# Up stage of a transformer block: the first weights in other places, the second feature-row set's first unit second, the second norm's subtractions on VectorE

## The chip, the cores and the metric

The kernel runs on one core of one Trainium2 chip. The metric is the device time in microseconds (us) of one execution. The engines are called as in the profile: PE is TensorE (matmuls), PEld its weight loads, DVE is VectorE, ACT is ScalarE, POOL is GpSimd, SP is SyncE, which here issues DMAs. Each engine works through its own instructions in order; between engines there are semaphores.

## The reference

One block with 2048 tokens of width 1024: a first norm and a mixer (two kinds of linear recurrences, in both directions), then a second norm and a feed-forward net whose gate half runs through a convolution of width 3 along the tokens. Everything is in float32. What matters here is the second half:

```
x = x + g1 * (mix_x @ w_out)
hx2 = rmsnorm(x, norm2_g) * (1.0 + sc2) + sh2
gate, up = split(hx2 @ w_up, 2)                 # 2 x 2816 columns
gate = sum(shift(gate, j) * conv_w[j]) + conv_b
x = x + g2 * ((silu(gate) * up) @ w_down)
out = rmsnorm(x, final_g)
```

## The kernel before

Products are made in float16 pairs: a float32 block is split into a high and a low half, and each product of two blocks is three matmuls (function `mm3`, lines 101 to 103). On top of that, the products of 2 x 2 blocks go by a Strassen-Winograd scheme with seven products instead of eight. So each set of features (of 1024 tokens) and each set of weights is held as seven blocks, numbered 0 to 6, each a pair.

The stages in order: `setup` and `heads` (the mixer), `out_proj`, `ffn_up`, `ffn_down`. The change touches the second and the third.

`out_proj` makes the second product and the second norm. Its four `out_product` calls each make 512 tokens of x, scale the rows by their root mean square (L1408, with the factor from a chain of small steps on GpSimd) and leave them in SBUF. Two of them make one feature-row set: `second_norm_a` takes the first 512 tokens of a set, `second_norm_b` the second 512. Both transpose on TensorE (L411), modulate on ScalarE (`modulated`, L1414), make block differences on VectorE (L1441) and split into a pair (`feat_pair`: the high half on ScalarE, L1417; the low half by a subtraction on the engine that is handed in, L1418). `second_norm_a` makes blocks 0 and 1 and keeps what the other blocks need; `second_norm_b` makes blocks 2 to 6. For the second set (t = 1) its two temporary rows lie in the four places with the tag q, and the rows it transposes lie in the places Q0, Q1, FG and KTt.

`ffn_up` runs over 11 pairs of column blocks (j). Each pair has two halves, ty = 0 (gate) and ty = 1 (up), and each half meets two feature-row sets t. One such meeting, (j, ty, t), is a unit (`ffn_unit`): seven products of 12 matmuls of 512 columns, in the order 0, 1, 5, 6, 4, 3, 2, with steps of the scheme's sums between them (ScalarE copies, L592; VectorE sums, L626). A gate unit's four results go through `gate_evac`: ScalarE's scale and bias (L1607), VectorE's two convolution steps (L1612, L1613) and the edges between the 512-token pieces (L1618, L1619). An up unit's go through `up_evac` (one VectorE step, L1632). `act_pairs` then splits the result into seven blocks and stores them in DRAM (L1642 to L1644).

The weights of a half are made by `up_weights(j, ty)`, a generator: load two raw blocks (L1521, two places with the tag wr); square them on ScalarE into the places of the last two blocks (L1528); sum the squares over rows on TensorE (L1533) and derive a power-of-two scale on VectorE; then seven steps, each with ScalarE's cast (L691) and VectorE's remainder (L692), with block differences on GpSimd (L536 to L545) between them. The seven blocks lie in places with the tag z, of which there are 14. The out projection's weights lie in 12 of these 14 until its last product is done. The tag vg (the mixer's value weights had it) has 7 places; later they hold parts of `down_blocks` and the outgoing pieces of `act_pairs`.

`ffn_unit` holds its sums in one buffer for t = 0 (tag ou0, a single place) and in two q places for t = 1. The results `act` of (j, t) lie in three pairs of places, taken in turn by 2j + t: K0 and K1, Q0 and Q1, FG and KTt.

The order is written by hand: while a unit's steps are traced, `work(n)` takes n steps from a list of background generators, `bg`. `ahead(u)` runs only the first step of a generator, its loads. The order in which the code is traced is a priority, not the order of execution: a scheduler with a simulated clock then puts each engine's instructions in a row, taking the first that it holds ready. Before, the units go (0,0,0), (0,0,1), (0,1,0), (0,1,1), (1,0,0), ..., and the list at the start of the up stage is second_norm_b of the second set, the loads of weights (0,1), and then weights (0,1) themselves.

Of the kernel before, what the change touches and what calls it, by code (L numbers as in the profile page):

```python
# [9 lines left out]
F32 = mybir.dt.float32  # L10
F16 = mybir.dt.float16
# [7 lines left out]
P = 128  # L19
# [3 lines left out]
G = 512  # L23
# [5 lines left out]
NJ = NF // 2  # L29
# [9 lines left out]
KEPT = ("K0", "K1", "Q0", "Q1", "FG", "KTt", "ou0")  # L39
# [11 lines left out]
def view(t, off, dims):  # L51
    return bass.AP(t.tensor, t.offset + off, [t.ap[0]] + dims)


class Kern:
# [286 lines left out]
    def modulation(self, cpool, pool, gain, sc, sh, dqcol, room=1.0):  # L342
# [5 lines left out]
        B = cpool.tile(shp, F32, name=f"B{dqcol}")  # L348
        U = pool.tile(shp, F32, tag="ra", bufs=4, name="modu")
        nc.vector.tensor_scalar(U, sc, 1.0, None, ALU.add)  # L350
        nc.vector.tensor_tensor(U, U, gain, ALU.mult)
        j = pool.tile(shp, F32, tag="ra", bufs=4, name="modj")
# [291 lines left out]

    def fm(self, W, X, n):

        def mm(ps, m, start, stop=True, w=None):
            w = W[m if w is None else w]
            for k in range(4):
                self.mm3(ps, lambda q: w[:, q, k], lambda q: X[m][:, k, q], start and k == 0, stop and k == 3)  # L650
        return mm, [P, n]

    def tm(self, W, X, n):

        def mm(ps, m, start, stop=True, w=None):
            w = W[m if w is None else w]
            for i in range(n // P):
# [26 lines left out]

    def pair_blocks(self, raws, W, s, neg, eng):

        nc = self.nc

        def emit(m, v):
            sc = neg if m == 3 else s  # L690
            nc.scalar.activation(W[m][:, 0], v, AF.Copy, scale=sc)  # L691
            nc.vector.scalar_tensor_tensor(W[m][:, 1], v, sc, W[m][:, 0], ALU.mult, ALU.subtract)  # L692
# [727 lines left out]
    def second_norm_a(self, t, xa):  # L1420

        place = (2, 4, 0, 3, 1, 5, 6) if t == 0 else (11, 12, 9, 8, 10, 7, 13)
        X = self.feats[t] = [None] * 7
        for m in (5, 3, 0, 1):
            X[m] = self.slot_tile([P, 4, 2, G], F16, f"y{place[m]}", "feat")
        self.held = [X[m].rearrange("p k a t -> p k (a t)").bitcast(F32) for m in (5, 3)]
        for k in range(4):
            for r in range(2):
                f = self.held[r][:, k]
                self.modulated(f, k + 4 * r, xa)  # L1430
                self.feat_pair(X[r][:, k], f, self.nc.gpsimd)
        self.rest = place

    def second_norm_b(self, t, xb):

        nc = self.nc
        X = self.feats[t]
        for m in (2, 4, 6):
            X[m] = self.slot_tile([P, 4, 2, G], F16, f"y{self.rest[m]}", "feat")
        pair = self.feat_pair  # L1440
        sub = lambda o, x, y: nc.vector.tensor_tensor(o, x, y, ALU.subtract)  # L1441
        for k in range(4):
            if t == 0:
                f = self.slot_tile([P, 2, G], F32, ("ou0", "FG", "KTt")[k % 3], "ftmp")
                b12, b22 = f[:, 0], f[:, 1]
            else:
                b12, b22 = (self.slot_tile([P, G], F32, "q", "ftmp") for _ in range(2))
            b11, b21 = (h[:, k] for h in self.held)
            self.modulated(b12, k, xb)
            self.modulated(b22, k + 4, xb)  # L1450
            yield
            sub(b11, b12, b11)
            pair(X[2][:, k], b22, nc.gpsimd)
            pair(X[4][:, k], b11, nc.vector)
            sub(b12, b22, b12)
            pair(X[6][:, k], b12, nc.gpsimd)
            sub(b22, b22, b11)
            sub(b12, b22, b21)
            pair(X[5][:, k], b22, nc.vector)
            pair(X[3][:, k], b12, nc.vector)  # L1460
            yield

    def out_proj(self):
        self.mod2 = self.modulation(self.cp, self.kp, self.sv[:, V_N2:V_N2 + 8], self.modT[:, 0, 32:40],
                                    self.modT[:, 0, 24:32], 1, 4.0)
        self.feats = [None, None]
        x0 = self.out_product(0)
        self.mixed_pairs(1)
        self.mixed_pairs(2)
        self.second_norm_a(0, x0)  # L1470
        x1 = self.out_product(1)
        self.mixed_pairs(3)
        for _ in self.second_norm_b(0, x1):
            pass
        x2 = self.out_product(2)
        self.ffn_setup()
        self.bg = [self.up_weights(0, 0)]
        self.work(99)
        self.second_norm_a(1, x2)
        x3 = self.out_product(3)  # L1480
        self.bg = [self.second_norm_b(1, x3)]


    def work(self, n):
# [29 lines left out]
    def up_weights(self, j, ty):  # L1514

        nc, kp = self.nc, self.kp
        wup = self.I["w_up"][0].rearrange("(k p) n -> p k n", p=P)
        raw = []
        for f in (j, j + NJ):
            r = self.slot_tile([P, KT, P], F32, "wr", "wur")  # L1520
            nc.sync.dma_start(r, wup[:, :, ty * FF + f * P:ty * FF + (f + 1) * P])  # L1521
            raw.append(r)
        yield
        W = [self.slot_tile([P, 2, 4, P], F16, "z", "w7") for _ in range(7)]
        ssq = kp.tile([P, 2], F32, tag="ssqw2", bufs=2, name="ssqw")
        sqs = [W[5 + i].rearrange("p a k n -> p (a k n)").bitcast(BF16) for i in range(2)]
        for i in range(2):
            nc.scalar.activation(sqs[i], raw[i].rearrange("p k n -> p (k n)"), AF.Square, scale=4.0, accum_out=ssq[:, i:i + 1])  # L1528
        yield
        col = self.ps("sc", [P, 2], "col")  # L1530
        for i in range(2):
            for k in range(KT):
                nc.tensor.matmul(col[:, i:i + 1], sqs[i][:, k * P:(k + 1) * P], self.onesb, start=k == 0 and i == 0,  # L1533
                                 stop=k == KT - 1 and i == 1, skip_group_check=True)
        s, neg, dq = self.scales(self.allsum16(ssq, "sc"), self.dqx[:, 1:2], ("dqz", "dqvg")[ty])

        if ty == 0:
            tap = kp.tile([P, 2, 3], F32, tag="taps", bufs=2, name="taps")
            nc.vector.tensor_scalar(tap, view(self.cw, j, [[NJ, 2], [NF, 3]]), dq, None, ALU.mult)
            row = kp.tile([P, 2], F32, tag="row", bufs=2, name="row")  # L1540
            nc.vector.scalar_tensor_tensor(row, col, 1.0 / 16, view(self.a2, j, [[NJ, 2]]), ALU.mult, ALU.mult)
            nc.vector.tensor_tensor(row, row, view(self.c2, j, [[NJ, 2]]), ALU.add)
            self.rows[j] = row
            self.W[j, 0] = W, tap
        else:
            row = self.rows.pop(j)
            q = kp.tile([P, 2], F32, tag="wdq", bufs=4, name="q")
            nc.vector.tensor_scalar(q, col, self.xx, 1.0, ALU.mult, ALU.mult)
            nc.vector.tensor_tensor(q, q, row, ALU.mult)
            nc.vector.tensor_tensor(q[:, 0:1], q[:, 0:1], q[:, 1:2], ALU.max)  # L1550
            sa, ia = self.pow2(kp, q[:, 0:1], 1, "a")
            nc.vector.tensor_copy(self.sas[:, j:j + 1], sa)
            nc.vector.tensor_copy(self.ias[:, j:j + 1], ia)
            self.W[j, 1] = W, dq
        yield

        yield from self.pair_blocks(raw, W, s, neg, nc.gpsimd)
# [90 lines left out]
    def ahead(self, steps):  # L1648

        next(steps)  # L1650
        yield

    def ffn_up(self):
        U = self.up_weights(0, 1)
        self.bg.append(self.ahead(U))
        for j in range(NJ):

            self.bg.append(U)
            act = [[self.slot_tile([P, 2 * G], F32, KEPT[2 * ((2 * j + t) % 3) + f], "act") for f in range(2)] for t in range(2)]
            ends = [{}, {}]  # L1660
            U = self.up_weights(j + 1, 0)
            for ty in range(2):
                if j + 1 < NJ and ty:
                    self.bg.append(U)
                    U = self.up_weights(j + 1, 1)
                    self.bg.append(self.ahead(U))
                for t in range(2):
                    evac = self.gate_evac(j, t, act, ends) if ty == 0 else self.up_evac(j, t, act)
                    for _ in self.ffn_unit(self.W[j, ty][0], self.feats[t], evac, t):
                        self.work(2)  # L1670
                    if ty == 0 and t == 0:
                        self.bg += [self.ahead(U)] * (j + 1 < NJ) + [self.down_blocks(j)]
                    if ty == 1:
                        self.bg.append(self.act_pairs(j, t, act[t]))
                if ty == 0:
                    self.work(99)
        self.work(99)

    def down_weights(self, m, n):
# [212 lines left out]
```

## Time and profile before

| | |
|---|---|
| time, median of 3 runs | 2640.04 us (2639.76 to 2642.20) |
| span of the profiled execution | 2636.4 us |
| mean granted TensorE clock | 0.981 |
| TensorE busy | 2515.8 us, 95% of the span |
| VectorE busy | 1887.8 us, 72% |
| ScalarE busy | 1349.2 us, 51% |
| GpSimd busy | 425.2 us, 16% |

The span goes from the first to the last instruction of one execution; no other time is listed for that execution. It is 3.6 us under the median. The matmuls overlap each other, so a share of busy time near 100% means that TensorE never waits, not that it could do nothing faster. The granted clock is a share of full speed: at 0.5 each matmul takes twice as long. In the profile the up stage's matmuls are those with feat and w as inputs, from 1391 us on, and those of the down stage are called pd, from 2226 us on.

### The profile page before, as it was taken

Reading aid. Unit: us, or ns where it says so; the run is one execution under the profiler, and the core shown is the slowest. Engines: PE = TensorE matmul, PEld = TensorE weight load, DVE = VectorE, ACT = ScalarE, POOL = GpSimd, SP = SyncE. Lnnn points to the kernel's source line nnn. Section 1 sums busy time; section 2 is a strip of 40 time slices with the busy share of each in tenths; the row PEclk is TensorE's granted clock in tenths of the full one; section 3 lists DMA queues with packets and bytes.
Section 4 is the critical chain, followed back from the end, with each engine's and each line's share of the span. In section 5 each row is a group of like instructions: output and inputs, shape, how many; then the busy total and the mean of one; then the engine's idle time right before and its main releaser. Section 6 shows DMA issues by size and latency. Waiting matters only on the chain. (4 is left out here: it accounts for less than half of the span.)

```text
span 2636.4 us, 56190 instructions
## 1 busy us (share of the span) xinstructions
PE 2515.8 (95%) x22763; PEld 1656.9 (63%) x22763; DVE 1887.8 (72%) x4275; ACT 1349.2 (51%) x2877; POOL 425.2 (16%) x409
## 2 busy tenths in 40 slices
PE   6799998999999999988998999999999999999998
PEld 3678887889899999984454444444444444444443
DVE  4888686786878778675558778888888887323656
ACT  5886466564654454453556556565555555211220
POOL 1100000000000000000354334343434433000000
PEclk7999999999999999998999999999999999999999
DMA  8324342441548567555421332333233236544552
GB/s 295 121 95 162 124 142 85 135 152 67 177 161 291 210 210 255 189 198 192 143 81 41 116 106 99 112 107 110 101 116 120 96 113 225 206 165 159 210 206 87
DMA packets 213621, 393.97 MB, mean 149 GB/s; under 512 B 15600, under 2 KB 97748, under 8 KB 208753
## 3 DMA queue, kind: packets, MB, share of 16 engines
q1 hardware_dynamic: 203808, 373.42, 40.8%
q10 hardware_dynamic: 9248, 16.79, 1.9%
q8 instruction: 178, 2.92, 0.5%
q14 instruction: 83, 0.67, 0.1%
q0 software_dynamic: 304, 0.17, 0.0%
HBM read 298.57 MB, written 91.75 MB: 148 GB/s over the span
## 5 line engine op out<-in xcount | busy, mean ns | idle before, releaser
L101 PE MATMUL pa<-feat,w 128*128 128x512 f16 x704 | 265.0, 381 | 7.6 <-ACT ta L592 5.6
L102 PE MATMUL pa<-feat,w 128*128 128x512 f16 x704 | 267.9, 381 | 0.0
L103 PE MATMUL pa<-feat,w 128*128 128x512 f16 x704 | 267.3, 380 | 0.0
L102 PE MATMUL pd<-wd,actl 128*128 128x512 f16 x616 | 233.3, 379 | 0.0
L103 PE MATMUL pd<-wd,actl 128*128 128x512 f16 x616 | 233.3, 379 | 0.0
L101 PE MATMUL pd<-wd,actl 128*128 128x512 f16 x616 | 232.6, 379 | 0.0
L102 PEld LDWEIGHTS <-w 128*128 128x128 f16 x1232 | 120.9, 98 | 150.9 <-issue 13.0
L103 PEld LDWEIGHTS <-w 128*128 128x128 f16 x1232 | 121.0, 98 | 147.0 <-issue 3.2
L101 PEld LDWEIGHTS <-w 128*128 128x128 f16 x1232 | 120.9, 98 | 141.9 <-issue 3.1
L102 PEld LDWEIGHTS <-hx 128*128 128x128 f16 x1824 | 179.4, 98 | 7.7 <-issue 5.9
L1407 POOL TENSOR_TENSOR ssq<-ssq 128x1 f32<-128x1 f32 x16 | 4.7, 292 | 1102.8 <-ACT junk L1405 1102.8
L101 PEld LDWEIGHTS <-hx 128*128 128x128 f16 x1824 | 179.9, 99 | 2.2
L103 PEld LDWEIGHTS <-hx 128*128 128x128 f16 x1824 | 179.6, 99 | 0.9
L1642 ACT ACTIVATE st<-act,modT 128x512 f16<-128x512 f32 x154 | 107.4, 717 | 109.6 <-DVE act L1632 64.1
L1643 DVE SCALAR_TENSOR_TENSOR st<-act,modT,st 128x512 f16<-128x512 f32 x154 | 140.3, 946 | 29.7 <-ACT st L1642 28.8
L101 PE MATMUL pa<-w_vg,hx 128*128 128x128 f16 x800 | 141.8, 219 | 1.1 <-ACT ct L592 0.7
L102 PE MATMUL pa<-w_vg,hx 128*128 128x128 f16 x800 | 141.7, 219 | 0.0
L103 PE MATMUL pa<-w_vg,hx 128*128 128x128 f16 x800 | 141.7, 219 | 0.0
L101 PE MATMUL pc<-feat,w 128*128 128x512 f16 x352 | 134.8, 383 | 2.2 <-ACT feat L1417 1.3
L103 PE MATMUL pc<-feat,w 128*128 128x512 f16 x352 | 135.2, 384 | 0.0
L102 PE MATMUL pc<-feat,w 128*128 128x512 f16 x352 | 135.0, 383 | 0.1
L101 PE MATMUL pa<-hx,w_z 128*128 128x256 f16 x464 | 127.0, 274 | 1.6 <-DVE K L634 1.3
(552 smaller groups left out, 7357.3 us busy)
## 6 DMA issues: line engine op xcount, KB each, us to landing
hx<-hxd SPq DMA_DIRECT2D x212, 512.0 KB, 4.7
actd<-st SPq DMA_DIRECT2D x154, 256.0 KB, 2.0
actl<-actd SPq DMA_DIRECT2D x28, 1024.0 KB, 5.0
wur<-in_w_up_dram SPq DMA_DIRECT2D x44, 512.0 KB, 3.8
raw<-in_w_in_dram SPq DMA_DIRECT2D x36, 512.0 KB, 4.7
wm<-in_w_mod_dram SPq DMA_DIRECT2D x64, 256.0 KB, 3.7
hxd<-hx SPq DMA_DIRECT2D x28, 512.0 KB, 3.9
wdb<-in_w_down_dram SPq DMA_DIRECT2D x44, 256.0 KB, 3.8
```

The lines of the kernel that those rows point to most:

```text
L101: mm(ps, lhs(0), rhs(0), start=start, stop=False, skip_group_check=True)
L102: mm(ps, lhs(0), rhs(1), start=False, stop=False, skip_group_check=True)
L103: mm(ps, lhs(1), rhs(0), start=False, stop=stop, skip_group_check=True)
L1407: nc.gpsimd.tensor_tensor(ssq[:, 0:1], ssq[:, 0:1], ssq[:, 1:2], ALU.add)
L1642: nc.scalar.activation(p[:, 0], v, AF.Copy, scale=s)
L1643: nc.vector.scalar_tensor_tensor(p[:, 1], v, s, p[:, 0], ALU.mult, ALU.subtract)
```

## The change

The first weights, (0, 0), lie in the vg places instead of z; all others stay in z. The loads of weights (1, 0) are traced before second_norm_a of the second set. In the up stage the units of the first two pairs go (0,0,0), (1,0,0), (0,0,1), (0,1,0), (0,1,1), (1,0,1), (1,1,0), (1,1,1); from the third pair on they go as before. The background list starts with weights (1, 0), then the loads of weights (0, 1), then second_norm_b; weights (0, 1) follow from the second unit on, the down blocks of pair 0 after the third unit, those of pair 1 after the sixth. All 32 low-half subtractions of the second norm that were GpSimd's are VectorE's: 16 in second_norm_a and 16 in second_norm_b.

```diff
@@ second_norm_a
-                self.feat_pair(X[r][:, k], f, self.nc.gpsimd)
+                self.feat_pair(X[r][:, k], f, self.nc.vector)
@@ second_norm_b
-            pair(X[2][:, k], b22, nc.gpsimd)
+            pair(X[2][:, k], b22, nc.vector)
             pair(X[4][:, k], b11, nc.vector)
             sub(b12, b22, b12)
-            pair(X[6][:, k], b12, nc.gpsimd)
+            pair(X[6][:, k], b12, nc.vector)
@@ out_proj
         self.bg = [self.up_weights(0, 0)]
         self.work(99)
+        self.u10 = self.up_weights(1, 0)
+        next(self.u10)
         self.second_norm_a(1, x2)
         x3 = self.out_product(3)
-        self.bg = [self.second_norm_b(1, x3)]
+        self.norm_b = self.second_norm_b(1, x3)
@@ up_weights
-        W = [self.slot_tile([P, 2, 4, P], F16, "z", "w7") for _ in range(7)]
+        W = [self.slot_tile([P, 2, 4, P], F16, "z" if j or ty else "vg", "w7") for _ in range(7)]
@@ ffn_up
-        U = self.up_weights(0, 1)
-        self.bg.append(self.ahead(U))
-        for j in range(NJ):
...
+        u10, u01 = self.u10, U(0, 1)
+        self.bg = [u10, ahead(u01), self.norm_b]
+        unit(0, 0, 0)
+        self.bg.append(u01)
+        unit(1, 0, 0)
+        u11 = U(1, 1)
+        self.bg.append(ahead(u11))
+        unit(0, 0, 1)
+        self.work(99)
+        self.bg.append(self.down_blocks(0))
+        unit(0, 1, 0)
+        unit(0, 1, 1)
+        self.work(99)
+        u20, u = U(2, 0), U(2, 1)
+        self.bg += [u11, ahead(u20)]
+        unit(1, 0, 1)
+        self.work(99)
+        self.bg += [u20, ahead(u), self.down_blocks(1)]
+        unit(1, 1, 0)
+        unit(1, 1, 1)
+        for j in range(2, NJ):
...
```

In the new code `unit(j, ty, t)` does what the inner loop's body did before: it takes the act places, runs `ffn_unit` with `work(2)` after each step, and puts act_pairs on the list after an up unit. The loop from j = 2 keeps the order of before.

More of the change, by code (lines that the diff above doesn't have):

```diff
@@ L1653, in ffn_up @@
     def ffn_up(self):
-        U = self.up_weights(0, 1)
-        self.bg.append(self.ahead(U))
-        for j in range(NJ):
[L1658 to L1676, printed above, removed]
+        acts, ends = {}, {}
@@ new lines, in unit @@
+        def unit(j, ty, t):
+            if ty == 0:
+                acts[j, t] = [self.slot_tile([P, 2 * G], F32, KEPT[2 * ((2 * j + t) % 3) + f], "act") for f in range(2)]
+            e = ends.setdefault(j, [{}, {}])
+            act = [acts.get((j, i)) for i in range(2)]
+            evac = self.gate_evac(j, t, act, e) if ty == 0 else self.up_evac(j, t, act)
+            for _ in self.ffn_unit(self.W[j, ty][0], self.feats[t], evac, t):
+                self.work(2)
+            if ty:
+                self.bg.append(self.act_pairs(j, t, act[t]))
@@ new lines, in ffn_up @@
+        ahead, U = self.ahead, self.up_weights
+        u10, u01 = self.u10, U(0, 1)
[13 more added lines that the diff above has]
+        self.bg += [u11, ahead(u20)]
@@ new lines, in ffn_up @@
+        unit(1, 0, 1)
[4 more added lines that the diff above has]
+        for j in range(2, NJ):
+            more = j + 1 < NJ
+            self.bg.append(u)
+            if more:
+                u = U(j + 1, 0)
+            unit(j, 0, 0)
+            self.bg += [ahead(u)] * more + [self.down_blocks(j)]
+            unit(j, 0, 1)
+            self.work(99)
+            if more:
+                self.bg.append(u)
+                u = U(j + 1, 1)
+                self.bg.append(ahead(u))
+            unit(j, 1, 0)
+            unit(j, 1, 1)
```

## The prediction

> **What bounds the kernel now.** I read the page first, then a table by stage around the change, then what TensorE (PE) waited for there, and at which instants.
>
> ```profile
> span 2636.4 us, 56190 instructions
> ...
> PE 2515.8 (95%) x22763; PEld 1656.9 (63%) x22763; DVE 1887.8 (72%) x4275; ACT 1349.2 (51%) x2877; POOL 425.2 (16%) x409
> ```
>
> TensorE is the bound, and the change leaves its matmuls as they are. So it can only win or lose time in which TensorE stands still or runs at a lower clock. The span is 3.6 us under the median of the runs (2640.04); I sum against the span and put these 3.6 us back at the end.
>
> ```profile
> core 0: us, PE busy (x) PEld busy (x) DVE busy (x) ACT busy (x) POOL busy (x), PEclk, DMA share, GB/s
> ...
> 1350.00:1396.00 46.00, 46.00 (x233) 23.30 (x232) 16.71 (x23) 20.15 (x39) 23.82 (x43) 1.00 0.17 64
> 1396.00:1419.00 23.00, 22.97 (x120) 12.07 (x119) 17.98 (x24) 16.52 (x30) 8.09 (x10) 1.00 0.12 35
> 1419.00:1435.00 16.00, 8.22 (x40) 3.12 (x38) 16.00 (x36) 9.75 (x19) 4.43 (x4) 0.68 0.00 1
> 1435.00:1465.00 30.00, 26.17 (x129) 11.48 (x128) 23.95 (x48) 20.09 (x37) 12.21 (x9) 0.94 0.29 97
> 1465.00:1519.00 54.00, 54.00 (x267) 24.76 (x266) 45.11 (x70) 29.08 (x54) 27.90 (x20) 1.00 0.34 113
> 1519.00:1529.00 10.00, 7.17 (x32) 2.66 (x30) 3.87 (x8) 5.10 (x9) 0.23 (x1) 0.66 0.48 155
> ...
> 1603.00:1676.00 73.00, 73.00 (x370) 33.56 (x369) 59.97 (x106) 43.22 (x76) 30.26 (x20) 1.00 0.32 109
> ```
>
> Columns: stage, its length, then busy time of each engine, the granted clock, DMA. Before 1396 and in the steady stage (1603:1676) TensorE has no idle time at all. The loss sits between 1419 and 1529: idle 7.78 + 3.83 + 2.83 = 14.4 us, and by the granted clock 0.32 x 8.22 + 0.06 x 26.17 + 0.34 x 7.17 = 6.6 us more. **21 us is the ceiling of what the change can win.** In 1419:1435 VectorE (DVE) is busy 16.00 of 16.00 us: there it is the bound.
>
> ```profile
> PE pa L101 <- ACT ta L592: 5.3, 1, 5.3
> PE col L1533 <- ACT w L1528: 4.5, 2, 2.6
> PE pa L101 <- DVE tb L626: 2.0, 1, 2.0
> PE pc L101 <- ACT feat L1417: 1.3, 1, 1.3
> ```
> ```profile
> 1391.24 0.38 PE L101 MATMUL pa<-feat,w 128*128 128x512 f16 x1
> 1391.46 0.38 PE L102 MATMUL pa<-feat,w 128*128 128x512 f16 x1
> ...
> 1420.95 0.38 PE L101 MATMUL pc<-feat,w 128*128 128x512 f16 x1 [1.25 <-ACT feat L1417]
> ...
> 1428.75 0.59 PE L101 MATMUL pa<-feat,w 128*128 128x512 f16 x1 [5.27 <-ACT ta L592]
> ...
> 1460.00 0.35 PE L1533 MATMUL col<-onesb,w 128*128 128x1 bf16 x8 [1.86 <-ACT w L1528]
> ...
> 1522.09 0.24 PE L1533 MATMUL col<-onesb,w 128*128 128x1 bf16 x3 [2.60 <-ACT w L1528]
> ```
>
> First the waits from 1391 to 1530, then the instants. The up stage begins at 1391.24; matmuls follow each other by 0.22 us, so a unit of 7 x 12 takes 18.1 us. I call the units A (0,0,0), B (0,0,1), C (0,1,0), E (1,0,0): weight pair, gate or up half, feature-row set. The first two stalls are the second norm: B needs the set that second_norm_b(1) is still making, so it is done too late for B. The 2.0 us are an evacuation that VectorE gave late. The last two stalls are column sums of weights whose squares came late.
>
> **The change, part by part.**
>
> ```profile
> L1418 POOL TENSOR_TENSOR feat<-feat x16: 1152/1158/1604, 1266.1 to 1374.7; 128x512 f16<-128x512 f32 x16
> L1418 POOL TENSOR_TENSOR feat<-ftmp,feat x16: 1156/1405/1758, 1313.1 to 1429.6; 128x512 f16<-128x512 f32 x16
> L1441 DVE TENSOR_TENSOR ftmp<-ftmp,feat x16: 674/678/1642, 1315.9 to 1432.6; 128x512 f32<-128x512 f32 x16
> L1418 DVE TENSOR_TENSOR feat<-ftmp,feat x16: 674/682/1653, 1320.6 to 1434.9; 128x512 f16<-128x512 f32 x16
> ```
> ```profile
> 1403.79 0.69 DVE L1441 TENSOR_TENSOR ftmp<-ftmp 128x512 f32<-128x512 f32 x1
> 1404.48 1.56 DVE L1418 TENSOR_TENSOR feat<-feat 128x512 f16<-128x512 f32 x1
> 1405.97 1.64 DVE L1441 TENSOR_TENSOR ftmp<-ftmp,feat 128x512 f32<-128x512 f32 x1
> ...
> 1404.01 3.05 POOL L1418 TENSOR_TENSOR feat<-ftmp,feat 128x512 f16<-128x512 f32 x2 [6.41 <-ACT feat L1417]
> ```
>
> (1) The subtractions. 32 leave GpSimd (POOL), where one takes 1.16 to 1.4 us, for VectorE, 0.68 each: 21.8 us more there. But beside a GpSimd subtraction a VectorE one takes 1.56 or 1.64 instead of 0.69, some 0.9 more. In second_norm_b(1), the only place where VectorE is the bound, 8 move: +8 x 0.68 = 5.4, and up to 8 x 0.9 = 7.2 comes back. Bounds +5.4 and -1.8; I take 0 to -1, since nearly every GpSimd subtraction there fell beside VectorE work. The other 24 lie before 1396, beside a TensorE that is fed without a break; cover gone, they would cost their net, 24 x (0.68 - 0.9 at most), about nothing. The Trainium skill speaks against this part: Perfetto Trace Analysis, Optimizing Scalar/DVE Operations, says that work may go from a saturated DVE to GPSIMD, and warns that a shared read port may take the help away. By its first half the sum would lose the 5.4 us; the lengthened rows are its second half, and I go by them.
>
> ```profile
> L626 DVE TENSOR_TENSOR tb<-pa,tb x6: 677/682/691, 1412.5 to 1526.7; 128x512 f32<-128x512 f32 x6
> L1612 DVE SCALAR_TENSOR_TENSOR act<-ta,taps,act x7: 736/743/1652, 1401.5 to 1517.4; 128x511 f32<-128x511 f32 x7
> L1618 DVE SCALAR_TENSOR_TENSOR act<-edge,taps,act x9: 202/214/1222, 1423.7 to 1519.7; 128x1 f32<-128x1 f32 x9
> ...
> 1349.34 0.15 DVE L113 TENSOR_SCALAR p2t<-p2t 128x1 int32<-128x1 int32 x1
> ...
> L1408 DVE TENSOR_SCALAR x<-x,rs_y x2: 753/754/755, 1385.8 to 1397.7; 128x1024 f32<-128x1024 f32 x2
> ...
> L692 DVE SCALAR_TENSOR_TENSOR w<-wur,p2s,w x24: 735/745/1834, 1383.8 to 1520.5; 128x512 f16<-128x512 f32 x24
> L691 ACT ACTIVATE w<-wur,p2s x24: 705/720/722, 1383.0 to 1516.5; 128x512 f16<-128x512 f32 x24
> L1528 ACT ACTIVATE w<-wur x10: 1039/1057/1057, 1321.3 to 1525.4; 128x1024 bf16<-128x1024 f32 x10
> L1521 SPq DMA_DIRECT2D wur<-in_w_up_dram x10: 379/383/384, 1317.3 to 1521.3; - x10
> ```
>
> (2) The places. The first weights are squared from 1321.3, but their blocks start only at 1383.0: their z places are those of the out projection's weights. In vg they can be made from about 1350, where VectorE is busy 16.7 of 46 us, ScalarE 20.2, GpSimd 23.8. That frees both raw places, and the loads of the second gate weights (moved ahead of the third product's row loads on SP's queue, and of the first up weights) land before 1391 and are squared. Their column sum and scale come after the last product, as its matmuls go first; so their blocks fall from about 1396, not earlier. A weight set costs VectorE 7 x 0.745 = 5.2, with its scalar steps (about ten of 0.15) and some three lengthenings by GpSimd's four subtractions (an estimate from the 0.9 above) about 10 us. One set is thus paid in free time instead of in the crowded stage.
>
> (3) The order, A E B C instead of A B C. TensorE gets 18.1 us (E) that don't need the norm. What is late next is VectorE's sum. A gate unit's evacuation is 3 x 0.68 + 8 x 0.743 + 4 x 0.21 = 8.8 us. The norm can't start before its last rows are scaled, at 1397.7 (L1408). VectorE's work from 1396 on: second gate weights 10, norm 36 x 0.68 = 24.5, A 8.8, first part of E 2.2: 45.5, so the norm ends at 1441.5. TensorE has A, E and three steps of B, 18.1 x 2 + 7.8 = 44 us, until 1435.2. **Stall about 6 us** where B had 9 (7.78 and its clock), and behind it C needs the first up weights: rest of E 6.6 and 10 of the set, half of it before C's first block, 1441.5 + 11.6 = 1453 against 1391.2 + 54.3 + 6 = 1451.5: **1.5 us more**. Two waits are added: E takes the one ta buffer (ou0) that A holds until its third evacuation, and E's act lies in the places (FG, KTt) of the rows that the norm is still transposing. Behind E's ACT step (L1607) nothing else may queue that the norm needs, or both stand; lower bound 0, upper bound the 5.3 us of the wait on ACT ta. I take 0, since the order on each engine is written by readiness, and keep 5 for the range. The first down blocks go behind B (their loads, SP's queue past the up weights', too); nobody waits for them in this stage.
>
> (4) Later. The second up weights have only unit (1,0,1) between their places and their use, 18 us for VectorE's 10: tight but enough. The down blocks no longer share unit (1,0,1) with them. Column sums stay in TensorE's order, so a late square still stops it: before, 1.86 and 2.60 us. I take one such stop, 2 us.
>
> Sum of after: 6 + 1.5 + 2 = 9.5 us, and with a lower clock behind one of them 0.5 more: 10, against 21. Span 2636.4 - 11 = 2625.4, time 2625.4 + 3.6 = **2629.0 us**. On the clock: here it fell behind 1.86 us of idle time too (0.94 in 1435:1465). TensorE: Matmul & The Clock Gate, Part 1, lets it fall after an idle window of about 3.4 us. By that rule short stops cost nothing more and after would be 0.5 us better; the trace disagrees.
>
> **The rivals.** R2, all is hidden: the scheduler fills E and B's steps so well that only a stop of 2 us is left: 2640 - 19 = 2621. For it: ScalarE is free (9.75 of 16) and VectorE only 45.1 of 54 us busy from 1465. Against: the 45.5 us above.
> R3, nothing gained: E's evacuations wait for the norm's transposes and the ou0 buffer, TensorE stands in E as it stood in B (7.8 + 2.6), and the late squares return elsewhere (6.7 and 4): 21 us again, 2640. For it: 5.3 us on ACT ta today is just such a wait. Against: a whole unit lies between.
> R4, slower: the first up weights are too late for C. Their load needs raw places that the second gate weights free only at about 1406, and their blocks stand behind the norm. If VectorE also does all of E and B first, they end at 1396 + 10 + 24.5 + 3 x 8.8 + 10 = 1467, C starts 16 to 21 us late, and with clock 0.66 behind a stop of that length (some 5 us) and the late squares the loss is 28: 2640 + 7 = 2647. It decides from about 1465 on for the last block. Against: the set is ahead of B's evacuations in the written order.
>
> **How the numbers follow.** R1 (forecast) 0.53, R2 0.14, R3 0.20, R4 0.13. What a measurement of this kernel can tell from no change is about 0.2%, 5.3 us. Faster by more: R1, less its upper edge (a loss over 15.8), and R2: 0.65. Same: R3 and that edge: 0.22. Slower: R4: 0.13. Range 2620 to 2642: from R2's full gain to a little above R3, leaving out R4 and a loss near zero. R1 alone: 2624 to 2634, from the 5 us kept either way.
>
> **What would show it.** In the trace of after: L1418 on VectorE alone, none near 1.6 us beside it in the norm; the first weights' L691 at about 1350 in place of 1383; TensorE at about 1411 going on with a unit of the first row set; one stall of 4 to 8 us near 1435 instead of 7.8 by then; all idle time from 1391 to 1530 under 10 us, clock near 0.97. Wrong if TensorE's longest wait is in E, or on blocks L692 of the first up weights, or if column sums wait longer than 4.5 us.

## The result: 4 us faster, a third of what was forecast

The changed kernel took 2637.35 us (median of 20 runs), the kernel before 2641.24 us in the same set: a ratio of 0.9984, interval 0.9977 to 0.9991, some 4 us. A second set of runs, the one that goes with the experiments below, gave 0.9988 (0.9977 to 0.9999). The forecast was a gain of 11 us, to 2629.0; the measured time lies in the range. The profiled execution took 2633.18 us with a span of 2631.4, against a span of 2636.4 before.

From the up stage on, line numbers are two higher in the changed kernel: L1530 and L1535 are the squares and the column sums (L1528 and L1533 before), L1614, L1615 and L1645 are the convolution steps and the remainders of act_pairs (L1612, L1613, L1643). On GpSimd, L536 to L545 are the differences of the up weights, L1576 those of the down blocks.

The page of the changed kernel, first its head, then the table by stage (columns as above):

```profile
span 2631.4 us, 56167 instructions
...
PE 2516.3 (96%) x22763; PEld 1657.9 (63%) x22763; DVE 1894.8 (72%) x4307; ACT 1347.6 (51%) x2877; POOL 383.0 (15%) x377
```
```profile
core 0: us, PE busy (x) PEld busy (x) DVE busy (x) ACT busy (x) POOL busy (x), PEclk, DMA share, GB/s
1396.00:1419.00 23.00, 23.00 (x121) 11.99 (x119) 22.16 (x32) 17.60 (x33) 6.52 (x4) 1.00 0.16 47
1419.00:1435.00 16.00, 14.83 (x89) 7.50 (x88) 16.00 (x31) 12.10 (x22) 0.00 (x0) 1.00 0.05 15
1435.00:1465.00 30.00, 25.87 (x113) 11.31 (x112) 29.71 (x58) 18.64 (x36) 11.65 (x8) 0.94 0.27 83
1465.00:1508.00 43.00, 43.00 (x216) 19.66 (x214) 27.46 (x50) 20.10 (x33) 12.86 (x10) 1.00 0.30 102
1508.00:1529.00 21.00, 15.97 (x73) 6.32 (x71) 18.65 (x29) 13.07 (x27) 10.95 (x7) 0.84 0.43 144
1529.00:1585.00 56.00, 56.00 (x275) 25.56 (x274) 44.95 (x76) 30.81 (x53) 25.17 (x18) 1.00 0.30 102
1585.00:1600.00 15.00, 12.59 (x73) 5.60 (x71) 8.67 (x22) 9.34 (x18) 3.61 (x3) 1.00 0.45 140
```

Where before TensorE was busy 8.22 of the 16 us from 1419, it is now busy 14.83. But idle time stands further down: 30.00 - 25.87 = 4.1 us in the fourth unit, 21.00 - 15.97 = 5.0 us in the seventh, 2.4 us after 1585, where before there was none. With the clock (0.06 x 25.87 + 0.16 x 15.97 = 4.1 us) and the 1.2 us of the second row, the loss is 16.8 us against the 21 of before. That is the gain of 4. The 2.4 us after 1585 fall in the tenth unit, (2,0,1). In 1435:1465 VectorE is busy 29.71 of 30 us, and right after it, from 1465 to 1508, only 27.46 of 43.

What TensorE waited for (engine, tile, line, releaser; total, times, longest), and then the instants:

```profile
PE pa L101 <- DVE tb L626: 4.1, 1, 4.1
PE pc L103 <- DVE w L692: 2.0, 1, 2.0
PE col L1535 <- ACT w L1530: 1.9, 2, 1.8
PE pa L101 <- ACT ta L592: 1.9, 1, 1.9
PE pa L103 <- DVE w L692: 1.3, 1, 1.3
PE allsum L132 <- ACT ftmp L1414: 1.2, 1, 1.2
```
```profile
1456.95 0.38 PE L101 MATMUL pa<-feat,w 128*128 128x512 f16 x1 [4.13 <-DVE tb L626]
...
1516.45 0.39 PE L103 MATMUL pc<-feat,w 128*128 128x512 f16 x1 [1.97 <-DVE w L692]
...
1518.12 0.39 PE L103 MATMUL pa<-feat,w 128*128 128x512 f16 x1 [1.28 <-DVE w L692]
...
1525.57 0.35 PE L1535 MATMUL col<-onesb,w 128*128 128x1 bf16 x8 [1.78 <-ACT w L1530]
```

The waits on the norm of 5.3 and 1.3 us are gone; 1.2 us on its ScalarE step (L1414) are left, at 1426, in the second unit. In their place stand waits on VectorE: a sum (L626) in the fourth unit, (0,1,0), 4.1 us where it was 2.0, and the remainders (L692) of weights (1,1) in the seventh, (1,1,0). The 1.9 us on a copy of ScalarE (L592) stand in the tenth.

### The profile page after: what moved, and what is told of

Read it like the earlier page. It is cut to its first block, busy times and chain, and to the rows that moved or that the text cites. A ratio compares the mean times of both kernels' runs of the same rounds, so it can differ in the third digit from the quotient of the medians.

```text
span 2631.4 us, 56167 instructions
## 1 busy us (share of the span) xinstructions
PE 2516.3 (96%) x22763; PEld 1657.9 (63%) x22763; DVE 1894.8 (72%) x4307; ACT 1347.6 (51%) x2877; POOL 383.0 (15%) x377
## 4 chain that ended last, share of the span: by engine, by line
PE 45%; DVE 5%; DMA 2%; issue 1%; ACT 1%; POOL 0%; SPq 0%; DVEq 0%; ACTq 0%; POOLq 0%
PE pd L103 5%; PE pd L101 5%; PE pd L102 5%; PE pa L101 5%; PE pa L102 5%; PE pa L103 5%; PE pc L101 2%; PE pc L102 2%; PE pc L103 2%; PE opp L101 2%; PE opp L103 2%; PE opp L102 2%; PE pb L101 1%; PE pb L102 1%; PE pb L103 1%
## 5 line engine op out<-in xcount | busy, mean ns | idle before, releaser
L1645 DVE SCALAR_TENSOR_TENSOR st<-act,modT,st 128x512 f16<-128x512 f32 x154 | 143.9, 968 | 29.3 <-ACT st L1644 28.9
```

The source lines that it names most:

```text
L1645: nc.vector.scalar_tensor_tensor(p[:, 1], v, s, p[:, 0], ALU.mult, ALU.subtract)
```

## The experiments

Two readings of the late stops stood against each other. **T1:** GpSimd's block differences lengthen VectorE's work where it is crowded. **T2:** the scale of weights (1,1) comes too late, since TensorE takes their column sum behind the fifth unit's matmuls. Besides, I took the change apart. The runs fall into three sets, each on another chip and with runs of the kernel before of its own, so times are compared within a set, and ratios across sets with their intervals in mind. "Upward stage" below is the time in the trace from its first matmul to the first of the downward stage: 834.8 us before, 831.1 changed. A ratio is always to the kernel before, with its interval; the delay is what TensorE is behind an even pace of 0.2157 us per matmul from the stage's start; it holds the clock and TensorE's own transposes and column sums as well as idle time. The expectations call (0,1,0) the third unit, which it was in the old order; in the new one it is the fourth, and my text says fourth.

### The stretched operations, in the trace of the changed kernel

VectorE's groups from 1390 to 1600 us (line, form, count | busy, mean ns of one | idle before):

```profile
L692 DVE SCALAR_TENSOR_TENSOR w<-wur,p2s,w 128x512 f16<-128x512 f32 x30 | 32.5, 1095 | 3.3 <-ACT w L691 3.3
L1645 DVE SCALAR_TENSOR_TENSOR st<-act,modT,st 128x512 f16<-128x512 f32 x28 | 28.7, 1038 | 11.5 <-ACT st L1644 11.5
L1615 DVE SCALAR_TENSOR_TENSOR act<-ta,taps,act 128x511 f32<-128x511 f32 x12 | 10.9, 909 | 0.0
...
L626 DVE TENSOR_TENSOR tb<-pa,tb 128x512 f32<-128x512 f32 x10 | 6.8, 683 | 9.1 <-PE pa L103 9.1
```

Now line L1615 alone over the whole upward stage (ns: shortest/median/longest):

```profile
L1615 DVE SCALAR_TENSOR_TENSOR act<-ta,taps,act x44: 736/743/1841, 1399.3 to 2188.7; 128x511 f32<-128x511 f32 x44
L1615 DVE SCALAR_TENSOR_TENSOR act<-pa,taps,act x22: 736/738/754, 1423.6 to 2193.6; 128x511 f32<-128x511 f32 x22
```

With ta, which lies in the core's working memory (SBUF), one takes up to 1841 ns. With pa, which lies in TensorE's own result memory, none takes more than 754, though 17 of the 22 ran beside a difference on GpSimd. So it is the operations with both inputs in SBUF that are stretched. Down to single ones, VectorE and GpSimd in the seventh unit:

```profile
1510.05 1.22 DVE L1621 SCALAR_TENSOR_TENSOR act<-edge,taps,act 128x1 f32<-128x1 f32 x1
1511.20 1.84 DVE L1645 SCALAR_TENSOR_TENSOR st<-act,modT,st 128x512 f16<-128x512 f32 x1
1512.96 5.10 DVE L692 SCALAR_TENSOR_TENSOR w<-wur,p2s,w 128x512 f16<-128x512 f32 x3
```
```profile
1511.23 1.26 POOL L1576 TENSOR_TENSOR wdb<-wdb 128x512 f32<-128x512 f32 x1
1512.46 1.71 POOL L545 TENSOR_TENSOR wur<-wur 128x512 f32<-128x512 f32 x1
1514.13 5.06 POOL L1576 TENSOR_TENSOR wdb<-wdb 128x512 f32<-128x512 f32 x3
```

Three remainders take 5.10 us, 1.70 each, while GpSimd's differences run beside them step for step. This agrees with the Trainium skill (SBUF — State Buffer, Who interferes with whom): a VectorE instruction with two SBUF inputs contends with a GpSimd one that reads SBUF, and what they share is an exclusive lock. The trace shows the lengthening and which forms it hits. It does not show that one waits for the whole of the other: a remainder (0.74 alone) and a difference (1.26 at its shortest) went by together in 1.70 us, less than their sum.

### All differences on VectorE; the scale early; both

The changed kernel once more, as the reference of this set:

> The changed kernel itself, as the reference of this set. Its upward stage took 831.1 us from its first matmul to the first matmul of the downward stage in the profile above, 3.7 us less than before. Both theories expect the same here: a stop of about 4 us in the third unit (1452.8 to 1457.0), three stops of 1 to 2 us in the seventh (1514.5 to 1525.6) with some 10 us of half clock, and a time 3 to 5 us under the kernel before.

2635.05 us, ratio 0.9988 (0.9977 to 0.9999), upward stage 830.5. The time and the stops are as expected. The half clock behind the seventh unit's stops is less than the 10 us expected: by the 0.84 of the table above it lasts 6.7 us (0.16 x 2 x 21). And in the seventh unit the delay grows by 7.5 us here and by 9.5 in the trace above, so two executions of one kernel differ by 2 us there.

```diff
# pair_blocks in up_weights; down_blocks likewise
-        yield from self.pair_blocks(raw, W, s, neg, nc.gpsimd)
+        yield from self.pair_blocks(raw, W, s, neg, nc.vector if j < 2 else nc.gpsimd)
```

> The changed kernel with every difference of the first two pairs' weight blocks (gate, up and down) made on VectorE instead of GpSimd. Theory T1 (VectorE's block additions are stretched from about 0.7 to 1.2 to 1.8 us each by GpSimd's differences running beside them): the stops at the third and the seventh unit shrink by more than the extra differences cost VectorE (about 0.7 each), and the time falls by 4 to 8 us under the changed kernel. Theory T2 (the seventh unit stops because the scale of its weights is made late, at 1496 to 1498, behind the fifth unit's matmuls in TensorE's order): the seventh unit's stops stay as they are, about 9.5 us with the half clock, and at most the third unit's 4 us go: 0 to 4 us gained. Rival T3 (VectorE is simply full, so work handed to it only adds): slower than the changed kernel by 3 us or more.

2629.50 us, ratio 0.9965 (0.9952 to 0.9977), upward stage 824.8: 6 us under the changed kernel. The stop in the fourth unit is gone:

```profile
1445.00:1460.00 15.00, 14.88 (x69) 6.66 (x68) 15.00 (x32) 11.00 (x23) 0.00 (x0) 1.00 0.29 93
```
```profile
PE 2515.7 (96%) x22763; PEld 1656.9 (63%) x22763; DVE 1892.6 (72%) x4331; ACT 1347.6 (51%) x2877; POOL 347.3 (13%) x353
```

VectorE executes 24 instructions more (4331 against 4307) and is not busy longer (1892.6 against 1894.8 us), while GpSimd loses 35.7 us. So T3 (VectorE is full, work handed to it only adds) falls. The delay grows by 4.3 us in the seventh unit, where in the changed kernel it grows by 7.5 to 9.5: T2 had these stops stay as they are. From there to 1740 it grows by some 12 us, with stops of up to 2.2 us (kernel before: 2, changed kernel: 5), so T1 doesn't explain all.

```diff
# up_weights, for (1, 1) alone: the squares get two vg places of their own,
# and the seven blocks' places W are taken only behind the scale
-        W = [self.slot_tile(... "w7") for _ in range(7)]
+        places = lambda: [self.slot_tile(... "w7") for _ in range(7)]
...
+        if apart:
+            W = places()
# ffn_up
-        self.bg.append(self.down_blocks(0))
+        self.bg += [self.down_blocks(0), ahead(u11), ahead(u11)]
         unit(0, 1, 0)
```

> The changed kernel with the column sum of the squares of weights (1,1) taken ahead of unit (0,1,0) in TensorE's order (the squares get places of their own, and the weights' seven blocks are asked for only after the scale), so that the scale is there some 25 to 30 us sooner. T2: VectorE starts the blocks as soon as places are free, the seventh unit's stops fall from about 5 us of idle time and 10 us of half clock to 1 or 2 us, and the time falls by 5 to 9 us under the changed kernel. T1: the additions are still stretched by GpSimd, wherever they lie, and the places come free no sooner: 0 to 2 us. A loss would mean that TensorE now waits for the squares at the earlier place.

2630.41 us, ratio 0.9966 (0.9953 to 0.9979), upward stage 825.0, some 5 us under the changed kernel (5.8 by the ratios, 4.6 by the medians). The stop in the fourth unit stays (4.12 us at 1456), and in the seventh the delay grows by 2.6 us instead of 7.5 to 9.5. First the sum behind the scale in TensorE's order (instants of the first and the last), in the changed kernel and in this one:

```profile
L132 PE MATMUL allsum<-both,onesb x2: 163/163/163, 1495.9 to 1525.8; 128*128 128x1 bf16 x2
```
```profile
L132 PE MATMUL allsum<-both,onesb x2: 163/163/163, 1472.7 to 1518.8; 128*128 128x1 bf16 x2
```

And two stages, first of the changed kernel, then of this one:

```profile
1460.00:1492.00 32.00, 32.00 (x147) 14.37 (x146) 17.89 (x29) 13.68 (x22) 5.73 (x4) 0.98 0.30 103
1492.00:1520.00 28.00, 24.75 (x127) 10.97 (x125) 26.57 (x41) 15.42 (x29) 18.08 (x12) 0.98 0.40 135
```
```profile
1460.00:1492.00 32.00, 32.00 (x156) 14.46 (x156) 23.93 (x46) 16.91 (x28) 8.80 (x7) 0.95 0.25 82
1492.00:1520.00 28.00, 26.67 (x139) 12.16 (x137) 21.58 (x27) 16.70 (x32) 14.55 (x11) 1.00 0.52 179
```

This is T2 in numbers. In the changed kernel VectorE stands free for 14 of 32 us and is then busy 26.57 of 28; with the scale 23 us sooner it does 6 us of that work in the free stretch. So T1 has the fourth unit's stop and T2 most of the seventh's; in the seventh they overlap, since T1's run had shortened its stops too. The edit also gives the squares places of their own; no run separates that from the earlier scale.

> Both edits together: all differences of the first two pairs on VectorE, and the scale of weights (1,1) early. If T1 and T2 hold for different stops (T1 the third unit, T2 the seventh), the gains add up: 8 to 12 us under the changed kernel, some 12 to 16 us under the kernel before. If one theory alone is right, this is no better than that theory's run. If VectorE is full (T3), it is slower than the scale's run alone by the cost of the differences, 3 us or more.

2619.91 us, ratio 0.9918 (0.9904 to 0.9932). By the ratios that is 21.6 us under the kernel before and about 18 under the changed kernel, where the two edits added up make 12; by the medians of this set it is 17.7 and 15, against 10. From five executions each, the surplus is hardly clear of the noise, but the traces have it too: the upward stage is 17 us shorter than the changed kernel's, and about 6 with either edit alone. TensorE's only idle stretch of over 0.2 us in the whole upward stage is 1.52 us, and the stage takes 813.6 us:

```profile
1396.00:1600.00 204.00, 202.25 (x1043) 94.99 (x1042) 177.25 (x346) 131.16 (x236) 48.80 (x39) 1.00 0.29 98
```

That the small late stops of the run with all differences on VectorE go too has a likely reason: the raw places of weights (1,1) come free sooner, and the squares of the next weights start at 1493.6 instead of 1520.7 in the changed kernel (1515.2 and 1504.2 with one edit alone). No run tests this link by itself.

### Which differences stretch

```diff
# down_blocks alone (the up weights' block differences stay on GpSimd)
-        sub = lambda o, x, y: nc.gpsimd.tensor_tensor(o, x, y, ALU.subtract)
+        eng = nc.vector if j < 2 else nc.gpsimd
+        sub = lambda o, x, y: eng.tensor_tensor(o, x, y, ALU.subtract)
```

> The changed kernel with only the down blocks' four differences of the first two pairs on VectorE; the up weights' block differences stay on GpSimd. T1: the four differences that ran beside the third unit's blocks (1447 to 1459) and the four beside the seventh's (1511 to 1519) stretched VectorE's additions by 0.5 to 1.1 us each; a third to a half of the 6 us that moving all differences gained goes with these, 2 to 4 us under the changed kernel. If it is the weights' own differences that stretch the blocks: 0 to 1 us. If VectorE is full: slower by 1 to 3 us.

2629.39 us, ratio 0.9970 (0.9959 to 0.9980), upward stage 827.2. That is 4 to 5 us under the changed kernel's ratio, at or over T1's upper edge: eight differences moved bring most of what 24 bring. The fourth unit's stop falls to 0.67 us.

```diff
# down_blocks, the differences of the first two pairs left out
+        sub = lambda o, x, y: ... if j > 1 else None
```

> The changed kernel without the down blocks' four differences of the first two pairs: these are left out, on any engine, so the down product of those pairs isn't the reference's. It takes GpSimd's work beside the third and the seventh unit away without giving VectorE any. T1 (stretching): the stop of 4.1 us at the third unit goes, as it did when VectorE took these differences (0.7 us left), and the upward stage falls from 831 to about 827 us or less. Rival (the gain of that run came from another order of instructions, not from the stretching): the stop stays above 2 us.

2627.62 us, ratio 0.9971 (0.9959 to 0.9984), upward stage 828.0. The time falls as T1 expects, but the fourth unit's stop only halves, to 2.15 us, and by the expectation a stop above 2 us speaks for the rival. The weights' own four differences still run there on GpSimd: with the down blocks' differences gone the remainders of that stretch still take 915 ns; they took 1121 in the changed kernel, and 738 with all differences on VectorE. The group from 1445 to 1460 in the changed kernel, and then in this one:

```profile
L692 DVE SCALAR_TENSOR_TENSOR w<-wur,p2s,w 128x512 f16<-128x512 f32 x4 | 4.5, 1121 | 0.0
```
```profile
L692 DVE SCALAR_TENSOR_TENSOR w<-wur,p2s,w 128x512 f16<-128x512 f32 x6 | 5.4, 915 | 0.0
```

So about half of that stop goes with the down blocks' differences. The other half stays open: in the run before this one the same four differences of the weights ran on GpSimd too, VectorE had four operations more, and the stop was 0.67 us. There VectorE's steps stand in another order beside them, so the rival (another order of instructions) may well have its part.

### The change taken apart

```diff
# part 3 alone on the kernel before: the three lines of the norm
-                self.feat_pair(X[r][:, k], f, self.nc.gpsimd)
+                self.feat_pair(X[r][:, k], f, self.nc.vector)
```

> The kernel before with part 3 alone: the second norm's 32 differences on VectorE. By the prediction's first part these go from 1.2 to 1.8 us beside GpSimd to about 0.7 each, the norm ends some 6 us sooner, and the stop of 5.3 us at the second unit falls with it. If the gain survives the later units: 3 to 6 us under the kernel before. If it is eaten by the later scale as in the changed kernel (T2): 0 to 2 us.

2631.28 us, ratio 0.9972 (0.9962 to 0.9983), upward stage 828.0: 32 subtractions moved bring 7 us, a little over the 3 to 6 expected and at least what the whole change brings.

```diff
# part 3 undone in the changed kernel
-                self.feat_pair(X[r][:, k], f, self.nc.vector)
+                self.feat_pair(X[r][:, k], f, self.nc.gpsimd)
```

> The changed kernel with part 3 undone: the norm's differences back on GpSimd, first weights in the value weights' places and the new order of units kept. The norm ends some 6 us later; the new order has one unit more ahead of it, so the second unit hardly waits, and the third unit's weights come later. If part 3 is what carries the gain: slower than the changed kernel by 2 to 6 us, at or over the kernel before. If the seventh unit's late scale sets the end whatever comes ahead of it (T2): within 2 us of the changed kernel.

2633.44 us, ratio 0.9988 (0.9979 to 0.9998), upward stage 830.2. As good as the changed kernel, as T2 expects: by the end of the fourth unit its delay is 12.3 us, that of the changed kernel 11.7, and in the seventh it loses 8.2 more.

```diff
# part 1 undone in the changed kernel
-        W = [self.slot_tile([P, 2, 4, P], F16, "z" if j or ty else "vg", "w7") for _ in range(7)]
+        W = [self.slot_tile([P, 2, 4, P], F16, "z", "w7") for _ in range(7)]
```

> The changed kernel with part 1 undone: the first weights lie in the weights' own places again, so that two sets of places stand between the first unit and the weights of the third. Their blocks can be made only when places come free, and the weights (0,1) come later than in the changed kernel: a longer stop at the third unit. By the prediction's second part: slower than the changed kernel by 3 to 8 us. If GpSimd's differences alone set the third unit (T1), about the same as the changed kernel.

2636.44 us, ratio 0.9998 (0.9989 to 1.0006): nothing gained on the kernel before, and 2.6 to 3.7 us behind the changed kernel (0.9988 and 0.9984 in its two sets; the intervals overlap). The delay shows where: 15.2 us by the end of the fourth unit against 11.7, as the prediction's second part has it. Later stops take some of that difference away again (upward stage 831.7, hardly more than the 831.1 and 830.5 of the changed kernel), so it lies at the lower edge of the 3 to 8 us expected.

```diff
# part 2 undone: the kernel before with part 3 and with
-        W = [self.slot_tile([P, 2, 4, P], F16, "z", "w7") for _ in range(7)]
+        W = [self.slot_tile([P, 2, 4, P], F16, "z" if j or ty else "vg", "w7") for _ in range(7)]
```

> The kernel before with parts 1 and 3 and without part 2: units in the old order, (0,0,0), (0,0,1), (0,1,0), (0,1,1), (1,0,0), ... . Theory T2': the new order is what makes the weights (1,1) late, since weights (1,0) hold their places from the second unit to the sixth and only one unit lies between the freeing of the places of (0,1) and the use of (1,1); in the old order two units lie there. Then this kernel waits for the norm at the second unit (about 10 us, as with part 3 alone) but has no stop at the seventh: 6 to 9 us under the kernel before, more than the whole change. Rival (the order is worth its 8 us and only later work eats it): no faster than the kernel before with part 3 alone, 0.9972 of it, and a stop at the seventh unit as well.

2633.61 us, ratio 0.9989 (0.9979 to 0.9999), upward stage 830.2. The seventh unit has no stop, as T2' expects (0.1 us of delay). But the time misses its 6 to 9 us: the sixth unit loses 7.3 us, at a wait on a convolution step of VectorE (1.55) and at a column sum whose square is late, with a lower clock behind them. First the norm's wait in the second unit, then that column sum:

```profile
1420.59 0.58 PE L101 MATMUL pc<-feat,w 128*128 128x512 f16 x1 [4.51 <-ACT feat L1417]
...
1513.38 0.23 PE L1533 MATMUL col<-onesb,w 128*128 128x1 bf16 x3 [2.71 <-ACT w L1528]
```

So the old order saves the seventh unit's stop and pays elsewhere. The rival was right in that this is no faster than part 3 alone.

Then the order and the places again, with the later work out of their way. The first kernel is the one before with part 3 and all differences of two pairs on VectorE; the second the one with both edits, but its first weights in z.

> The kernel before with part 3, and with all block differences of the first two pairs on VectorE too; first weights in z, units in the old order. It tells what the new order and places are worth once GpSimd is out of the way. T1 and T2 together: the old order keeps the wait for the norm (10 us of lag at the second unit, which moving differences can't shorten, since GpSimd does little there), so this ends 5 to 10 us behind the changed kernel with both edits (0.9918 of before): about 0.995 to 0.996. Rival (the order is worth nothing, only GpSimd's differences cost time): within 2 us of that kernel.

2626.35 us, ratio 0.9962 (0.9947 to 0.9977), upward stage 821.8: a little over the 0.995 to 0.996 that T1 and T2 together expect, within the interval. It is behind the kernel with both edits by 8 us in the upward stage and by 12 by the ratios. Its delay grows by 10.6 us in the second unit, the wait for the norm.

> The changed kernel with both edits (all differences of the first two pairs on VectorE, scale of weights (1,1) early), but with the first weights back in z, so without part 1. If part 1 is what makes the new order possible: the third unit's stop returns and this is 4 to 8 us slower than with part 1. If its worth has gone once VectorE's additions aren't stretched: within 2 us.

2629.57 us, ratio 0.9967 (0.9956 to 0.9979), upward stage 824.5: 11 us behind the kernel with both edits in the upward stage and 13 by the ratios, more than the 4 to 8 expected. The one stop that was expected to return doesn't; TensorE waits in small steps again, 9.6 us in all, from 1444 on. So the new places and order, which add nothing to part 3 in the change as it was made, are worth some 8 to 12 us once VectorE isn't stretched and the scale comes early, and the order needs the places for it.

## Why the prediction was wrong in size

Its frame held in two points: the matmuls are unchanged, and no kernel here gained clearly more than the ceiling of 21 us. That all losses lie before 1530 held for the kernel before alone: the changed kernel loses 2.4 us after 1585. The step that failed is (4), the late stops.

**Step (1) held in its durations.** In the changed kernel all subtractions of the norm are at their short form, and its block differences but one (1.76 us, at 1404, beside a difference of the weights on GpSimd):

```profile
L1418 DVE TENSOR_TENSOR feat<-ftmp,feat x16: 678/684/690, 1407.3 to 1440.4; 128x512 f16<-128x512 f32 x16
L1441 DVE TENSOR_TENSOR ftmp<-ftmp,feat x8: 680/683/689, 1408.5 to 1436.9; 128x512 f32<-128x512 f32 x8
```

The norm ends at about 1441, the forecast's 1441.5. What I took for 0 to -1 us was worth 7 us of the kernel as an edit alone: 3 us of delay less by the middle of the second unit, and the rest in shorter stops up to the sixth. Why those get shorter no run here shows. In the changed kernel it was worth nothing (0.9988 with it and without).

**Step (2) held**: the first weights' blocks start at 1346.8 (L691), the second gate weights' at about 1396. **Step (3) held in size, not in place.** Forecast 6 us in B, the unit that waits for the norm, and 1.5 in C; measured 1.2 us in E, nothing in B, and 4.1 with 1.6 of clock in C, 6.9 against 7.5. B in the changed kernel:

```profile
1431.94:1450.07 18.13, 18.13 (x86) 8.23 (x85) 17.84 (x47) 12.66 (x27) 2.53 (x3) 1.00 0.21 59
```

B starts 41.9 us behind A, where the sum had 36.2: it left out the norm's transposes and the column sums, which TensorE makes between the matmuls of A and E (all but the 1.2 us of idle time). The norm, done at 1441 as forecast, then came in time for B; that is read from the trace, no run tests it. VectorE, busy for 45.7 of the 46 us from 1419, was behind with the evacuations instead, and C waited for a sum. Of the 4.1, the runs put half or more down to GpSimd's down-block differences, which the prediction had waved through as work for which nobody waits. They are waited for by no one, but they go with longer VectorE steps beside them.

**Step (4) failed.** It put the second up weights at nothing ("18 us for VectorE's 10: tight but enough") and set one stop of 2 us for a late square. The late square came as forecast, 1.8 us. But the blocks of these weights stopped TensorE for 2.0 and 1.3 us more, the clock took 2.6 in place of 0.5, and 2.4 us after 1585 stood in no term: 10 us in all against 2.5, and that is the whole miss. The 10 us of VectorE counted these weights alone. In the 28 us from 1492 VectorE is busy 26.57: it also evacuates two units and makes the pieces of act_pairs (7.5 us), and the six main remainders take 9.1 us where at 0.74 each they'd take 4.5:

```profile
L692 DVE SCALAR_TENSOR_TENSOR w<-wur,p2s,w 128x512 f16<-128x512 f32 x6 | 9.1, 1534 | 0.0
L1645 DVE SCALAR_TENSOR_TENSOR st<-act,modT,st 128x512 f16<-128x512 f32 x6 | 7.5, 1263 | 0.8 <-ACT st L1644 0.8
```

And the scale wasn't there when the places came free: its column sum stands behind the fifth unit's matmuls in TensorE's order, at 1495.9 (the row above), though the squares were done by 1479:

```profile
L1530 ACT ACTIVATE w<-wur x2: 1057/1058/1060, 1470.8 to 1478.0; 128x1024 bf16<-128x1024 f32 x2
```

In step (2) I had used just this rule ("their column sum and scale come after the last product"), and not again here.

**The rivals.** R3 named the right end, "the late squares return elsewhere", with too large a bill. R2's time, 2621, is what the kernel with both edits reaches: the order and places can hide it all, once VectorE isn't stretched and the seventh unit is fed. R4's late first up weights never stopped TensorE: C lost 6 us with the clock, not 28, and waited for a sum. On the clock, the trace spoke for the prediction's choice in that short stops do cost: behind those of 1.3 to 2.0 us in the seventh unit it fell again (0.84), and so it did behind one of 2.02 us in the run with all differences on VectorE:

```profile
1492.00:1520.00 28.00, 25.98 (x128) 11.46 (x127) 26.73 (x56) 18.75 (x36) 5.42 (x4) 0.94 0.49 159
```

The Trainium skill (TensorE: Matmul & The Clock Gate, Part 1) has the clock fall after an idle window of about 3.4 us; here less was enough. But the length of a stop alone doesn't decide: the clock stayed at 1.00 behind the single 1.52 us of the kernel with both edits, behind 1.9 us at 1592 in the changed kernel (row 1585:1600), and behind 2.0 us at 1446 in the kernel before (1.00 from 1448 to 1458), the same kernel in which it fell behind 1.86. What decides, no run here shows.

## What to carry to other kernels

When a change moves a unit ahead, list for every later unit which places its weights wait for, when their scale can be made, and all that VectorE does in that stretch, not only the new work; here the loss moved to stretches where that sum was full. A reduction on the engine that bounds the kernel is placed by its position in that engine's order: issue it one unit early if the inputs are there. And helpers beside a crowded engine are priced by what they do to it: here GpSimd's 24 differences cost VectorE about as much time as doing them itself.

## What was not expected of the hardware

Steps of 128x1 whose inputs lie in SBUF are stretched by as much as large ones: an edge step (L1621) took 1.22 us beside GpSimd, against about 0.21 alone. And 24 operations given to VectorE took nothing off its free time in the sum of a whole execution: 1892.6 us busy with them, 1894.8 without.
